# Macaron encoder on one core: the first operands of an FFN's second projection formed ahead of the last gate, and the joining copies moved one product later

## The chip, the cores and the metric

The kernel runs on one core of a Trainium2 chip. The metric is the time of one execution on the device in microseconds (us), lower is better. The core has five engines that run side by side, each through its own instructions in order: TensorE (PE in the profile; its weight loads are PEld), VectorE (DVE), ScalarE (ACT), GpSimd (POOL) and SyncE (SP), which issues DMAs. They wait for each other through semaphores.

## The reference

Two layers, each with two half-step FFNs around a mixer, then a final norm; all in float32, for 512 tokens of width 1024.

```python
def swiglu(x, w_in, w_out):            # w_in 1024 x 5632, w_out 2816 x 1024
    gu = x @ w_in
    g, u = jnp.split(gu, 2, axis=-1)
    return (jax.nn.silu(g) * u) @ w_out

for l in range(DEPTH):                 # DEPTH = 2
    x = x + 0.5 * swiglu(rms_norm(x, ffn1_norm[l]), ffn1_w_in[l], ffn1_w_out[l])
    x = x + mixer(rms_norm(x, mix_norm[l]), ...)
    x = x + 0.5 * swiglu(rms_norm(x, ffn2_norm[l]), ffn2_w_in[l], ffn2_w_out[l])
return rms_norm(x, final_norm)
```

So there are four FFN stages. The change touches these alone.

## The kernel before, in words

**Numbers as halves.** Every float32 operand is split into a high part and a low part that the tensor engine can take, and a product is three matmuls: high x high (L491 in the profile), low x high (L492), high x low (L494). A weight granule arrives by DMA as `raw` (128 x 1024). ACT copies it to its high half `whi` (L191, or L186 where the sign is turned), DVE subtracts to get the low half `wlo` (L194, L187). `whi` and `wlo` have three buffers each, so the making of a half waits until PE has read an older one. `ws.next()` hands a granule to a product and prepares those two places ahead. Weight loads are issued on SP eight granules ahead; some get a second weight added to them by a POOL DMA or by DVE (L164).

**Seven products instead of eight.** Matrix products are taken in 2 x 2 blocks by a Strassen scheme. In the first projection an FFN has five blocks of columns (`jb` 0 to 4). A block runs seven products on PE in this order, each two granules of 12 matmuls: A (operand 1), B (5), A (6), C (2), A (7), B (3), A (4). Between them ACT copies results from PSUM (`snap`, L561, tiles `sn`) and DVE subtracts (`less`, L566). `gate` forms the SwiGLU gate for one half of the tokens: ACT's tanh (L722, tiles `th`), one DVE product (L723); `times` (L729) multiplies by the other projection. `z1` is the gated tile of token half 0, ready behind the last product; `z2` that of half 1, ready a little before it.

**Turning.** The second projection needs the gated tiles with columns and rows exchanged. `halves` lets ACT copy a gated tile as 16-bit words into a buffer `zs` (two copies, L681) and SP issue a DMA transpose into `zt` (L682); the pair is put on the list `turned`. `joined` takes the first of the list and lets ACT copy its words from `zt` into a tile `at` (L698): two copies of 128 x 1024, or, where a block's four column tiles fall into two chunks, two of 128 x 256 and two of 128 x 768. The two tiles of a block are joined in the next block; those of the last block in the second projection.

**The second projection.** `at` has twelve tiles: two halves, two token halves, three chunks of 3, 4 and 4 column tiles. The list `steps` names 21 products on PE (tiles `o`), by operand 1 (three chunks), 2 (three), then for each chunk 5, 6, 7, 3, and last 4 (three). `make(i)` forms the operand of step i once: where a difference or sum of `at` tiles is needed DVE forms it in place (L742), ACT copies the high part `c1h`, `c2h`, ... (L321), DVE subtracts the low part `c1l`, ... (L322). Step i's loop pass calls `make(i)` and `make(i + 1)` ahead of its product and `make(i + 2)` behind it. Operands 1 of the first two chunks are made of tiles that the earlier blocks have filled; those of step 5 (operand 2, last chunk) and later need the last block's tiles. `update` (L748) adds finished products to x.

**Order.** Inside a stage most instructions are put in order by a scheduler that follows the order of the Python calls and the engines' estimated times; a place in the code is therefore a place in a priority order, and the built order can differ from it by a few instructions. Three of the four stages (all but the second) also load ACT's table for the square root at the end of the first projection.

Of the kernel before, what the change touches and what calls it, by code (L numbers as in the profile page):

```python
# [37 lines left out]
NB = 5  # L38
# [52 lines left out]
def encoder_kernel(  # L91
# [29 lines left out]
    def pair(s="ps"):  # L121
        return [bank(s), bank(s)]
# [373 lines left out]
    def product(ps, acts, kts, start, stop=True, again=False, hook=None, by_block=False, ahead=AHEAD):  # L496

        h, l, off = acts  # L500
        n = (len(kts) + 1) // 2

        def granule(i, w, b):
            res = []
            for k, kt in enumerate(kts[2 * i : 2 * i + 2]):
                c, z = slice(off + b * P, off + (b + 1) * P), slice(k * T, (k + 1) * T)
                res.append((
                    ps[b], h[:, kt, c], l[:, kt, c], w[0][:, z], w[1][:, z], start and i + k == 0,
                    stop and 2 * i + k == len(kts) - 1,
                ))  # L510
            return res

        if by_block:
            w = [ws.next() for _ in range(n)]
            for b in range(2):
                for i in range(n):
                    late_low(granule(i, w[i], b), again)
            return
        for i in range(n):
            w = ws.next(AHEAD if i < n - 1 and ahead else ahead)  # L520
            if i < n - 1:
                late_low(granule(i, w, 0) + granule(i, w, 1), again)
            else:
                late_low(granule(i, w, 0), again)
                late_low(granule(i, w, 1), again)
            if hook and i == 0:
                hook()
# [36 lines left out]
    def less(ps, t):  # L564
        for b in range(2):
            res = V.tensor_tensor(t[:, b, :], ps[b], t[:, b, :], ALU.subtract)  # L566
        return res
# [30 lines left out]
    def stage_ffn(norm, nxt, late):  # L598
# [75 lines left out]
        late_at, turned = [], []  # L674
# [12 lines left out]
        def joined():  # L687

            t, j, f0 = turned.pop(0)
            q = 0  # L690
            while q < 4:
                h, c, i = PLACE[f0 + q]
                n = 1
                while q + n < 4 and PLACE[f0 + q + n] == (h, c, i + n):
                    n += 1
                to = at_tile(h, j, c).bitcast(U16).rearrange("p i (t w) -> p w i t", w=2)
                for w in range(2):
                    S.activation(to[:, w, i : i + n, :], t[:, w, q : q + n, :], AF.Copy)  # L698
                q += n
# [163 lines left out]
        for jb in range(0 if first else 1, NB):  # L863
            f0 = 2 + 4 * jb
            if first and jb == 0:
                with tc.manual_schedule(engines={mybir.EngineType.DVE, mybir.EngineType.Activation}):
                    pa = pair("A")
                    product(pa, acts[1], K4, True)
                    for j in range(2):
                        t = snap(pcl[j])  # L870
                        pcl[j] = [t[:, 0, :], t[:, 1, :]]
                    s1 = snap(pa)
                    second(s1)
                    pb = pair("B")
                    product(pb, acts[5], K4, True)
                    sb = snap(pb)
                    norm.rstd()
            else:
                pa, pb, s1, sb = two(jb)
                settle_at()  # L880
                joined()
            product(pa, acts[6], K4, False, again=True)
            s2 = snap(pa)
            settle_at()
            if turned:
                joined()
            if jb or not first:
                second(s1)
            else:
                plain_out()  # L890
            z1 = gate(s1, 0)
            product(pa, acts[7], K4, False, again=True)
            less(pa, sb)
            product(pb, acts[3], K4, False, again=True)
            less(pb, s2)
            z2 = gate(s2, 1)
            times(z2, [sb[:, 0, :], sb[:, 1, :]], 1)
            halves(z2, 1, f0)
            if jb == NB - 1:
                make(0)  # L900
                make(1)
            product(pa, acts[4], K4, False, again=True)
            times(z1, pa, 0)
            halves(z1, 0, f0)
# [4 lines left out]
        for i, (m, c, _) in enumerate(steps):  # L909
            make(i)  # L910
            if i:
                make(i + 1)
            key = {6: 1, 4: 7}.get(m, m)
            if key not in ps:
                ps[key] = pair(f"o{key}")
            if m == 4 and c == 0 and nxt.mix:
                make(i + 2)
                ws.finish_stage()
                swap_pools(1)
            product(  # L920
                ps[key], made.pop(i), list(range(len(CHUNK[0][c]))), c == 0 and m in (1, 2, 3, 5, 7), c == 2,
                m in (4, 6), by_block=late and i == len(steps) - 1,
            )
            if i == 0:
                settle_at()
            if i == 1:
                turned.reverse()
                joined()
            if i == 3:
                joined()  # L930
            if m == 4 and c == 0 and not late:
                with tc.manual_schedule(engines={mybir.EngineType.DVE, mybir.EngineType.Activation}):
                    make(i + 2)
                    nxt.quad(1, 1)
                    if nxt.mix:
                        nxt.low01 = nxt.quad_high(0, 1)
                    else:
                        nxt.quad(0, 1)
            make(i + 2)
            if i == 6 and not late:  # L940
                nxt.quad(0, 0)
            if m == 4 and c == 1:
                update(ps[1], 1, 0, 1)
            if m == 4 and c == 0 and late:
                gf[0] = slot(F32, "gf", (D,))
                nc.sync.dma_start(out=gf[0], in_=bass.AP(tensor=gfin.tensor, offset=gfin.offset, ap=[[0, P], [1, D]]))
            if c < 2:
                continue
            if m == 1:
                update(ps[1], 0, 0, -1)  # L950
            elif m == 2:
                update(ps[2], 0, 0, 1)
                nxt.squares(0, 0)
            elif m == 5:
                update(ps[5], 0, 1, 1)
                update(ps[5], 1, 1, -1)
            elif m == 6:
                update(ps[1], 1, 1, 1)
            elif m == 7:
                update(ps[7], 1, 1, 1)  # L960
                nxt.squares(1, 1)
                update(ps[1], 0, 1, -1)
            elif m == 3:
                update(ps[3], 0, 1, 1)
                nxt.squares(0, 1)
                if late:
                    make(i + 3)
            elif late:
                with (
                    tc.issue_after(ws.items[-1].last.ins),  # L970
                    tc.manual_schedule(engines={mybir.EngineType.DVE, mybir.EngineType.Activation}),
                ):
                    ready = nxt.inverses(2)
                    next(ready)
                    gained(2, 0)
                    next(ready)
                    gained(2, 1)
                    for _ in ready:
                        pass
                    scaled(nxt, 2)  # L980
                    update(ps[7], 1, 0, 1, (0,))
                    nxt.squares(1, 0, (0,))
                    root = [nxt.inverse(b, *nxt.terms(b)) for b in range(2)]
                    next(root[0])
                    gained(3, 0)
                    gained(3, 1)
                    scaled(nxt, 3)
                    update(ps[7], 1, 0, 1, (1,))
                    nxt.squares(1, 0, (1,))
                    next(root[1])  # L990
                    next(root[0])
                    gained(0, 0)
                    next(root[0])
                    gained(0, 1)
                    scaled(nxt, 0)
                    next(root[1])
                    next(root[1])
                    whole(nxt, 1, 0)
                    whole(nxt, 1, 1)
            else:  # L1000
                update(ps[7], 1, 0, 1)
                if not nxt.mix:
                    nxt.squares(1, 0)
                nxt.later((1, 0))
# [978 lines left out]
```

## Time and profile before

| | |
|---|---|
| median of 3 runs | 1891.07 us (1890.44 to 1891.85) |
| the profiled execution | 1892.1 us |
| its span, first to last instruction | 1890.3 us |
| PE busy | 1860.5 us |
| DVE busy | 1641.4 us |
| ACT busy | 1310.0 us |
| mean granted clock of TensorE | 0.994 |

How to read it: times of a view are counted from the start of the span. A row of a timeline gives start, duration, engine, line, operation, what it writes and reads, shapes and how many such instructions the row joins; in brackets stands the idle time of that engine before it and what ended it. Matmuls overlap, so the distance between starts tells more than a duration. A row of stretches gives the stretch, its length, the busy time of PE, PEld, DVE, ACT and POOL with instruction counts, the granted clock, the DMA share and GB/s. A row of the waits gives who waited for whom, us in total, times, and the longest.

### The profile page before, as it was taken

The numbers are of one execution on the slowest core, as the hardware profiler recorded it, in microseconds if no ns is written. First come the engines' busy times: TensorE is split into PE (matmuls) and PEld (weight loads), VectorE is DVE, ScalarE is ACT, GpSimd is POOL, SyncE is SP. The second block draws the span as 40 slices with busy tenths as digits, with TensorE's granted clock in tenths as the row PEclk, the third lists the DMA queues.
The fourth block names the chain that finished last, engine by engine and source line by source line (L and its number), as shares of the span: only waits on it lengthen the run. The fifth ranks groups of instructions, "written<-read, shape, count | busy, mean of one in ns | idle before, by whom it ended". The sixth has DMA issues, their size and how long they took to land. (4 is left out here: it accounts for less than half of the span.)

```text
span 1890.3 us, 24637 instructions
## 1 busy us (share of the span) xinstructions
PE 1860.5 (98%) x8830; PEld 1549.5 (82%) x8830; DVE 1641.4 (87%) x2006; ACT 1310.0 (69%) x1788; POOL 171.3 (9%) x210
## 2 busy tenths in 40 slices
PE   9999999999999999999999999999999999999998
PEld 7888788888888888878888877888888888888786
DVE  7878899788989988879998878998989899887898
ACT  6777775668666767776667767666685576777764
POOL 0101011100111101001010100101001101000010
PEclk9999999999999999999999999999999999999999
DMA  9898799832886788879888886989248867888794
GB/s 299 223 244 202 194 254 280 213 104 93 249 224 163 182 211 231 206 201 265 251 186 226 209 211 181 267 265 211 84 134 232 214 172 175 229 215 206 197 273 153
DMA packets 190140, 393.70 MB, mean 208 GB/s; under 512 B 95489, under 2 KB 95617, under 8 KB 190017
## 3 DMA queue, kind: packets, MB, share of 16 engines
q1 hardware_dynamic: 161344, 293.77, 48.6%
q0 software_dynamic: 28528, 98.33, 28.9%
q8 instruction: 69, 1.13, 0.2%
q14 instruction: 55, 0.44, 0.1%
q10 hardware_dynamic: 144, 0.02, 0.0%
HBM read 365.85 MB, written 2.11 MB: 195 GB/s over the span
## 5 line engine op out<-in xcount | busy, mean ns | idle before, releaser
L194 DVE TENSOR_TENSOR wlo<-raw,whi 128x1024 fp32r<-128x1024 f32 (+1 forms) x534 | 631.1, 1195 | 166.8 <-ACT whi L191 165.7
L191 ACT ACTIVATE whi<-raw 128x1024 fp32r<-128x1024 f32 (+1 forms) x534 | 546.9, 1036 | 299.5 <-DVE raw L164 56.9
L150 POOL DMA_DIRECT2D raw<-in_wst_dram x166 | 144.3, 888 | 1400.5 <-DMA raw<-in_wst_dram 722.2
L164 DVE TENSOR_TENSOR raw<-raw,raw 128x1024 f32<-128x1024 f32 (+1 forms) x150 | 179.1, 1196 | 2.2
L492 PE MATMUL A<-whi,xl 128*128 128x512 f32 x400 | 155.7, 389 | 0.0
L491 PE MATMUL A<-whi,xh 128*128 128x512 f32 x400 | 155.7, 389 | 0.0
L698 ACT ACTIVATE at<-zt 128x1024 uint16<-128x1024 uint16 (+2 forms) x96 | 110.9, 1172 | 17.7 <-DMA zt<-zs 17.5
L186 ACT ACTIVATE whi<-raw 128x1024 fp32r<-128x1024 f32 (+1 forms) x83 | 86.0, 1037 | 48.5 <-PE A L492 21.5
L494 PE MATMUL A<-wlo,xh 128*128 128x512 f32 x400 | 115.0, 389 | 0.0
L187 DVE SCALAR_TENSOR_TENSOR wlo<-raw,whi 128x1024 fp32r<-128x1024 f32 (+1 forms) x83 | 98.6, 1197 | 15.5 <-ACT whi L186 15.3
L722 ACT ACTIVATE th<-sn,rh 128x512 f32<-128x512 f32 x80 | 55.7, 718 | 46.4 <-DVE sn L566 45.8
L494 PEld LDWEIGHTS A<-wlo,xh 128*128 128x128 f32 x400 | 75.1, 188 | 15.6
L491 PEld LDWEIGHTS A<-whi,xh 128*128 128x128 f32 x400 | 75.1, 188 | 15.4
L492 PEld LDWEIGHTS A<-whi,xl 128*128 128x128 f32 x400 | 75.1, 188 | 15.4
L491 PE MATMUL C<-whi,xh 128*128 128x512 f32 x208 | 82.1, 395 | 4.3 <-ACT whi L191 4.3
L492 PE MATMUL C<-whi,xl 128*128 128x512 f32 x208 | 81.7, 393 | 0.0
L492 PE MATMUL B<-whi,xl 128*128 128x512 f32 x208 | 81.0, 389 | 0.0
L491 PE MATMUL B<-whi,xh 128*128 128x512 f32 x208 | 80.9, 389 | 0.0
L681 ACT ACTIVATE zs<-th 128x1024 uint16<-128x1024 uint16 x80 | 79.6, 1043 | 0.4 <-DVE th L729 0.4
L561 ACT ACTIVATE sn<-A 128x512 f32<-128x512 f32 x104 | 59.3, 587 | 10.3 <-PE A L494 9.9
L494 PE MATMUL C<-wlo,xh 128*128 128x512 f32 x208 | 60.5, 393 | 0.0
L494 PE MATMUL B<-wlo,xh 128*128 128x512 f32 x208 | 59.8, 389 | 0.0
(449 smaller groups left out, 4790.3 us busy)
## 6 DMA issues: line engine op xcount, KB each, us to landing
raw<-in_wst_dram SPq DMA_DIRECT2D x470, 512.0 KB, 5.9
raw<-in_wst_dram POOLq DMA_DIRECT2D x174, 512.0 KB, 8.3
raw<-in_wst_dram SPq DMA_DIRECT2D x30, 256.0 KB, 3.5
bm<-in_bias_dram SPq DMA_DIRECT2D x16, 384.0 KB, 3.7
vs<-v SPq DMA_DIRECT2D x12, 256.0 KB, 3.8
x<-in_xin_dram SPq DMA_DIRECT2D x4, 512.0 KB, 10.2
raw<-in_wst_dram POOLq DMA_DIRECT2D x8, 256.0 KB, 8.1
dft<-in_dft_dram POOLq DMA_DIRECT2D x8, 256.0 KB, 4.4
```

The lines of the kernel that those rows point to most:

```text
L150: G.dma_start(out=self.t, in_=wst[GRAN_AT[self.plus]][:, 0 : self.n], accum_op=ALU.add)
L164: V.tensor_tensor(self.raw.t, self.raw.t, self.add.t, ALU.add)
L186: S.activation(hi, t, AF.Copy, scale=-1.0)
L187: self.last = V.scalar_tensor_tensor(lo, t, -1.0, hi.bitcast(F32), ALU.mult, ALU.subtract)
L191: S.activation(hi[:, cs], t[:, cs], AF.Copy)
L194: self.last = V.tensor_tensor(lo[:, cs], t[:, cs], hi[:, cs].bitcast(F32), ALU.subtract)
L491: PE.matmul(ps, lh, rh, start=start, stop=False, skip_group_check=again)
L492: PE.matmul(ps, ll, rh, start=False, stop=False, skip_group_check=again)
L494: PE.matmul(ps, lh, rl, start=False, stop=stop, skip_group_check=again)
L561: S.activation(t[:, b, :], ps[b], AF.Copy)
L681: S.activation(s[:, h], words[:, h], AF.Copy)
L698: S.activation(to[:, w, i : i + n, :], t[:, w, q : q + n, :], AF.Copy)
```

## The change

The call of `joined()` that stood behind the second product of a block is gone; the one behind the third product stays (it joins the first turned tile now), and a new one stands behind the fifth product, for the second tile. In the last block `make(0)` and `make(1)`, the operands of the first two steps of the second projection, move from behind `halves(z2, ...)` to ahead of `gate(s2, 1)`. The last block's two tiles are joined at steps 2 and 5 of the second projection instead of 1 and 3.

```diff
             else:
                 pa, pb, s1, sb = two(jb)
                 settle_at()
-                joined()
             product(pa, acts[6], K4, False, again=True)
             s2 = snap(pa)
             settle_at()
...
             z1 = gate(s1, 0)
             product(pa, acts[7], K4, False, again=True)
+            if turned:
+                joined()
             less(pa, sb)
             product(pb, acts[3], K4, False, again=True)
             less(pb, s2)
+            if jb == NB - 1:
+                make(0)
+                make(1)
             z2 = gate(s2, 1)
             times(z2, [sb[:, 0, :], sb[:, 1, :]], 1)
             halves(z2, 1, f0)
-            if jb == NB - 1:
-                make(0)
-                make(1)
             product(pa, acts[4], K4, False, again=True)
             times(z1, pa, 0)
             halves(z1, 0, f0)
...
             if i == 0:
                 settle_at()
-            if i == 1:
+            if i == 2:
                 turned.reverse()
                 joined()
-            if i == 3:
+            if i == 5:
                 joined()
```

## The prediction

> **What bounds the kernel now.** I read the page's first part, then who waited for whom on PE, then the timeline around the longest waits, then busy time by stretch of time.
>
> ```profile
> PE 1860.5 (98%) x8830; PEld 1549.5 (82%) x8830; DVE 1641.4 (87%) x2006; ACT 1310.0 (69%) x1788; POOL 171.3 (9%) x210
> PE o L491 <- ACT c1h L321: 13.5, 4, 3.4
> PE C L491 <- ACT whi L191: 4.3, 4, 2.3
> PE o L492 <- DVE c1l L322: 0.5, 2, 0.3
> ```
>
> PE is busy 98% of the span, so only its waits can be won. There are two families of four, one per FFN stage: the start of the second projection (o) waits for its first operand c1h, 13.5 us together, and a product C in the first projection waits for a weight half, 4.3 us. First one end of a first projection, on PE:
>
> ```profile
> 216.01 0.39 PE L491 MATMUL A<-whi,xh 128*128 128x512 f32 x1
> 218.73 0.39 PE L491 MATMUL A<-whi,xh 128*128 128x512 f32 x1
> 221.00 0.61 PE L494 MATMUL A<-wlo,xh 128*128 128x512 f32 x2
> 224.99 1.14 PE L491 MATMUL o<-whi,c1h 128*128 128x512 f32 x2 [3.37 <-ACT c1h L321]
> 229.55 0.40 PE L491 MATMUL o<-whi,c1h 128*128 128x512 f32 x1
> 222.00:226.00 4.00, 1.01 (x3) 0.44 (x3) 3.02 (x5) 4.00 (x6) 0.00 (x0) 0.89 0.47 158
> 226.00:232.00 6.00, 6.00 (x22) 4.90 (x22) 5.97 (x6) 5.97 (x7) 0.00 (x0) 0.79 1.07 227
> ```
>
> The last two rows are stretches of time; the figure behind the five busy times is the granted clock (0.89, 0.79). A granule of 12 matmuls takes 218.73 - 216.01 = 2.72 us. PE stands still for 3.37 us, and the 12 matmuls behind the wait take 229.55 - 224.99 = 4.56 us, because the clock is granted at half for a while. One end costs 3.37 + 1.84 = 5.2 us, four cost 20.8.
>
> Why c1h is late is seen on ACT, which works in order:
>
> ```profile
> 206.26 1.34 ACT L722 ACTIVATE th<-sn,rh 128x512 f32<-128x512 f32 x2 [0.32 <-DVE sn L566]
> 210.37 1.06 ACT L191 ACTIVATE whi<-raw 128x1024 fp32r<-128x1024 f32 x1 [1.81 <-issue]
> 212.58 1.06 ACT L191 ACTIVATE whi<-raw 128x1024 fp32r<-128x1024 f32 x1 [1.15 <-PE B L492]
> 221.25 1.06 ACT L186 ACTIVATE whi<-raw 128x1024 fp32r<-128x1024 f32 x1 [2.54 <-PE A L492]
> 222.21 1.99 ACT L681 ACTIVATE zs<-th 128x1024 uint16<-128x1024 uint16 x2
> 224.10 1.78 ACT L321 ACTIVATE c1h<-at 128x768 fp32r<-128x768 f32 x2
> 225.78 1.99 ACT L681 ACTIVATE zs<-th 128x1024 uint16<-128x1024 uint16 x2
> 227.79 1.28 ACT L907 ACT_TABLE_LOAD   x1
> 229.09 0.20 ACT L907 ACTIVATE sq<-ones 128x1 f32<-128x1 f32 x1
> 230.15 1.04 ACT L321 ACTIVATE c1h<-at 128x1024 fp32r<-128x1024 f32 x1
> 233.90 2.58 ACT L698 ACTIVATE at<-zt 128x1024 uint16<-128x1024 uint16 x2
> ```
>
> The two c1h, 1.78 us, stand behind the zs copies of the last gated tile, which itself is ready only when the product ends. They read tiles of earlier blocks.
>
> **The change part by part.**
>
> *Operands 0 and 1 ahead of the last gate.* In the built order the c1h now stand before the weight halves of the block's last product, their c1l on DVE directly behind the second `less`. The two at copies of the second turned tile (2.58 us) are also put into this stretch, from one product earlier. What hides these 4.4 us: ACT idles 1.81 + 1.15 us there, and the half started at 210.37 ends at 211.43 and is used at 216.01. Laid in a row behind th (ending 207.6): at, weight half, at, first c1h to 211.8, weight half to 212.8. Its lead shrinks from 4.6 to 3.2 us: no stall. If that cover were gone, each further us is a us of PE. On DVE:
>
> ```profile
> 213.68 1.23 DVE L194 TENSOR_TENSOR wlo<-raw,whi 128x1024 fp32r<-128x1024 f32 x1 [0.99 <-ACT whi L191]
> 217.28 1.23 DVE L187 SCALAR_TENSOR_TENSOR wlo<-raw,whi 128x1024 fp32r<-128x1024 f32 x1 [0.38 <-ACT whi L186]
> 224.97 0.96 DVE L322 TENSOR_TENSOR c1l<-at,c1h 128x768 fp32r<-128x768 f32 x1 [0.94 <-ACT c1h L321]
> 225.96 0.96 DVE L742 TENSOR_TENSOR at<-at,at 128x768 f32<-128x768 f32 x1
> 226.83 1.22 DVE L322 TENSOR_TENSOR c1l<-at,c1h 128x1024 fp32r<-128x1024 f32 x1
> 227.97 3.35 DVE L742 TENSOR_TENSOR at<-at,at 128x768 f32<-128x768 f32 x3
> ```
>
> The c1l (0.87 + 1.14 us from start to next start) fall into a stretch with idle gaps like those in the first two rows; carried along the order, the last gate's products on DVE end some 0.5 us later than now. All four waits of 3.37 us and their slow granules go: **20.8 us**.
>
> *What is late next.* The third c1h and c1l. PE would begin the projection at 221.45 (two matmuls of 0.227 us after 221.00) and need them after granules of 2.72, 1.36, 2.72 and 2.72 us, at 230.97; its built order starts with two matmuls of the high part, so the low part is needed at 231.4. ACT, in its new order: zs of z2 to 224.1, two weight halves to 226.45, zs of z1 to 228.35, table load and sq to 229.75, c1h to 230.8. DVE: behind the last gate's weights, the four subtractions L742 (4.0 us) and two weight lows end at 230.8, c1l at 232.1. A stall of 0.7 us. In the second FFN stage there is no table load, but one weight half and its low part stand ahead of c1l: 1.8 us. Three times 0.7 and once 1.8: **-3.9 us**. Whether 1.8 us of waiting brings the half clock is open: rows below bound it, 1.17 us without and 2.32 us with it; I take no half clock, as nearer to the first, and keep 1.84 us for the range. [...]
>
> [...]
>
> *The second projection can give some back.* DVE is nearly full there, and in the third stage its low halves already come just in time:
>
> ```profile
> 1180.00:1246.00 66.00, 66.00 (x297) 54.73 (x296) 63.25 (x64) 40.86 (x49) 8.63 (x10) 1.00 0.91 258
> 1792.00:1858.00 66.00, 66.00 (x293) 54.66 (x292) 64.75 (x65) 40.03 (x46) 8.59 (x10) 1.00 0.92 261
> 1251.07 1.23 DVE L194 TENSOR_TENSOR wlo<-raw,whi 128x1024 fp32r<-128x1024 f32 x1
> 1252.35 1.21 PE L494 MATMUL o<-wlo,c3h 128*128 128x512 f32 x4
> 313.19 1.23 DVE L194 TENSOR_TENSOR wlo<-raw,whi 128x1024 fp32r<-128x1024 f32 x1
> 315.69 0.61 PE L494 MATMUL o<-wlo,c3h 128*128 128x512 f32 x2
> ```
>
> DVE is busy 63.25 and 64.75 of 66 us (the third busy time). PE cannot come earlier than DVE does, plus the lead: 1.27 us in the first stage (314.42 to 315.69), 0.05 in the third. DVE itself comes earlier by the two c1l and the gap before them less the delay: 2.0 + 0.94 - 0.5 = 2.4 us, up to 3.8 with its small gaps. That lets the first stage keep its 4.5 us (5.2 - 0.7). The third keeps about 3.2, the fourth, with as full a DVE, I set alike: **-2.5 us**.
>
> *The at copies one product later.* In ordinary blocks they only change places with other copies: nothing. In the block behind the one whose tiles are split over two chunks:
>
> ```profile
> 1093.81 0.50 ACT L698 ACTIVATE at<-zt 128x256 uint16<-128x256 uint16 x1 [3.04 <-DMA zt<-zs]
> 1096.03 1.06 ACT L698 ACTIVATE at<-zt 128x768 uint16<-128x768 uint16 x1
> 1096.93 2.01 ACT L191 ACTIVATE whi<-raw 128x1024 fp32r<-128x1024 f32 x2
> 1098.04 0.50 PE L491 MATMUL C<-whi,xh 128*128 128x512 f32 x1 [2.32 <-ACT whi L191]
> 1711.24 0.50 PE L491 MATMUL C<-whi,xh 128*128 128x512 f32 x1 [1.17 <-ACT whi L191]
> 1090.00:1105.00 15.00, 12.68 (x49) 9.97 (x48) 6.78 (x6) 10.91 (x16) 0.00 (x0) 0.89 0.56 142
> ```
>
> ACT stands in line for a turned tile, then two long copies and two snaps come ahead of the weight half for C. The built order keeps the wait (the 256-wide copies stay), but puts the half before both long copies and the second snap: it comes 1.85 us sooner. The longest C wait falls from 2.32 to 0.5, its half clock goes (0.11 x 15 = 1.7 us), the other three, 4.3 - 2.3 = 2.0 us, vanish: 1.85 + 1.7 + 2.0 = **5.5 us**. Joining at steps 2 and 5 instead of 1 and 3 moves 2.58 us on ACT twice, before tiles that are needed steps later: nothing. On SP one weight load now stands between the last two transposes, and the later loads wait for a zs that ends 0.6 us later; they are fetched eight granules ahead: nothing.
>
> *Sum:* 20.8 - 3.9 - 2.5 + 5.5 = 19.9 us. The profiled execution took 1892.1 us (span 1890.3); less 19.9 is 1872.2. The median of the runs is 1.03 us lower: **1871**.
>
> **The rivals.**
>
> *Everything is kept* (DVE and ACT keep pace): 20.8 + 0.2 for c1l + 5.5 = 26.5 us, 1864.5. For it: what DVE lacks is under 2 us an end. Against: the 0.05 us lead.
>
> *DVE becomes the bound.* If the c1l only displace other DVE work ahead of the gate, DVE wins just its 0.94 us gap, and PE that plus its lead: 2.2 us in the first stage, the same assumed for the second, 1.0 in the other two, 6.4 in all, with 5.5 for C 11.9 us: 1879. If C gains only half, 1882. For it: 63 to 65 of 66 us busy. Against: the idle gaps before the gate.
>
> *Nothing to measure:* the built order puts the c1h where the text says, so this needs losses that happen to cancel the gains: 1891.
>
> *Slower.* Place: DVE's order ahead of the third c1l, where the four subtractions and the weight lows now stand. If that c1l comes x us after PE needs it, an end loses x + 1.84 (half clock again) for the 20.8 + 5.5 = 26.3 us won over four ends; it decides from x = 26.3 / 4 - 1.84 = 4.7 us. I work out 0.7 and 1.8. At x = 6 the kernel takes 1891 + 4 x 7.84 - 26.3 = 1896. For it: DVE has no idle left there. Against: no row makes 4 us more.
>
> **How the numbers follow.** Forecast 0.55; all kept 0.15; DVE bound 0.18; nothing 0.05; slower 0.07. A measurement of this kernel can tell about 0.2%, 3.8 us. The first three are faster by more: 0.88. The range takes these three with their ends: 1864 to 1882; what is left out is 0.12. The 1.84 us of the second stage lie inside.
>
> **What would show it.** Right: PE's waits for c1h gone, the granted clock full at each start of a second projection; a wait of PE for c1l of 0.5 to 2 us, longest in the second stage; C waits under 1 us; short waits of PE for wlo in the second projections of the third and fourth stage. Wrong: a wait of over 2 us at the third operand, PE waiting for wlo by several us (DVE bound), or a wait in the last two products of a first projection (ACT too full).

## The result, and the profile after

| | before | changed |
|---|---|---|
| median | 1890.76 us (1889.64 to 1891.85) | 1871.08 us (1869.66 to 1872.91) |
| the profiled execution | 1892.1 us | 1872.9 us |
| its span | 1890.3 us | 1871.1 us |
| ratio of the times | | 0.990, 95% 0.988 to 0.991 |

Faster by 1.0%, 19.7 us; 19.9 us were forecast, for 1871. The profiled execution of the changed kernel is the longest of its four (the other three spans were 1867.9 to 1869.4).

The profile's first part and the waits of PE, changed kernel:

```profile
PE 1854.5 (99%) x8830; PEld 1543.7 (82%) x8830; DVE 1638.3 (88%) x2006; ACT 1307.7 (70%) x1788; POOL 171.4 (9%) x210
```
```profile
PE A L491 <- ACT sn L561: 1.9, 2, 1.1
PE o L492 <- DVE c1l L322: 1.6, 3, 0.5
PE o L494 <- DVE wlo L194: 1.0, 2, 0.7
PE o L491 <- ACT c2h L321: 1.0, 1, 1.0
PE C L491 <- ACT whi L191: 0.5, 1, 0.5
```

The family c1h (13.5 us) is gone, the family C is down from 4.3 us to one wait of 0.5. In their place stand small waits: for the third operand (c1l, three times 0.5), for a weight's low half, and for the second family of operands (c2h, once). One start of a second projection, on PE, with the stretch around it:

```profile
220.73 0.62 PE L494 MATMUL A<-wlo,xh 128*128 128x512 f32 x2
221.19 0.39 PE L491 MATMUL o<-whi,c1h 128*128 128x512 f32 x1
223.91 0.39 PE L491 MATMUL o<-whi,c1h 128*128 128x512 f32 x1
```
```profile
221.00:227.00 6.00, 6.00 (x28) 4.99 (x27) 6.00 (x8) 5.60 (x6) 0.00 (x0) 1.00 0.62 180
```

No idle time, 2.72 us for the granule instead of 4.56, the granted clock 1.00.

Both kernels run 8830 matmuls, so the two traces can be laid over each other: start of PE's k-th matmul before, less that of the k-th after. Read over the stages, this shift tells where the 19.2 us of the spans came from (gain +, loss −):

| shift gained in stage | 1 | 2 | 3 | 4 | sum | forecast |
|---|---|---|---|---|---|---|
| around the product C | −0.35 | +0.6 | +4.1 | +1.4 | +5.7 | +5.5 |
| start of the second projection | +5.2 | +5.8 | +5.6 | +5.4 | +22.0 | +20.8 |
| third and fourth operand | −0.7 | −1.0 | −0.85 | −0.75 | −3.3 | −3.9 |
| given back later in the second projection | −2.3 | 0 | −2.15 | −0.26 | −4.7 | −2.5 |

The rest, −0.55 us, is +0.65 in the first 10 us of the span, and −0.8 and −0.4 where the two mixers begin: PE waits there for 0.75 and 1.10 us (the row "A <- sn" above; the kernel before had one such wait, of 0.86 us).

So the total was right, but not every term: the starts and C won a little more than worked out, and nearly twice as much was given back. Where the first stage gave it back is seen behind its third operand, on ACT, DVE and SP's queue in turn:

```profile
228.26 1.28 ACT L908 ACT_TABLE_LOAD   x1
229.55 0.20 ACT L908 ACTIVATE sq<-ones 128x1 f32<-128x1 f32 x1
229.66 1.05 ACT L321 ACTIVATE c1h<-at 128x1024 fp32r<-128x1024 f32 x1
232.29 1.04 ACT L191 ACTIVATE whi<-raw 128x1024 fp32r<-128x1024 f32 x1
236.51 1.37 ACT L698 ACTIVATE at<-zt 128x1024 uint16<-128x1024 uint16 x1 [3.17 <-DMA zt<-zs]
237.75 0.61 ACT L191 ACTIVATE whi<-raw 128x512 fp32r<-128x512 f32 x1
```
```profile
230.74 1.22 DVE L322 TENSOR_TENSOR c1l<-at,c1h 128x1024 fp32r<-128x1024 f32 x1 [0.65 <-ACT c1h L321]
238.39 0.69 DVE L194 TENSOR_TENSOR wlo<-raw,whi 128x512 fp32r<-128x512 f32 x1 [3.29 <-ACT whi L191]
```
```profile
224.26 5.09 SPq L682 DMA_TRANSPOSE zt<-zs  x1
229.44 0.53 SPq L148 DMA_DIRECT2D raw<-in_wst_dram  x1
230.07 3.38 SPq L682 DMA_TRANSPOSE zt<-zs  x1
```

ACT comes to the first joining copy at 233.3 and stands there 3.17 us for the turned tile (the list is reversed, so the tile that is joined first is the one turned last). The weight half behind it is 3.2 us late, and DVE idles 3.29 us for that half. In the kernel before, the copy at 233.90 did not wait at all: PE's stall had put ACT behind the transposes. Then, the two transposes stood back to back in the queue:

```profile
224.48 5.43 SPq L682 DMA_TRANSPOSE zt<-zs  x2
```

Here the one weight load between them, forecast at nothing, is in the way. In all four stages ACT stands for that tile, 3.17, 2.26, 1.06 and 0.80 us.

That standing alone does not give the size of what a stage loses (2.3, 0, 2.15 and 0.26 us). DVE's idle time for weight halves in the first 69 us of each second projection follows the loss better: it goes from 0.2, 0.3, 1.7 and 1.2 us in the kernel before to 3.6, 0.9, 3.7 and 1.1. In the third stage only 1.16 of the 3.7 us stand right behind the tile. The other 2.5 us stand behind two halves for which ACT waited for a weight load, as the 1.7 us of the kernel before do:

```profile
1204.71 1.06 ACT L191 ACTIVATE whi<-raw 128x1024 fp32r<-128x1024 f32 x1 [1.98 <-DMA raw<-in_wst_dram]
1208.75 2.01 ACT L191 ACTIVATE whi<-raw 128x1024 fp32r<-128x1024 f32 x2 [2.03 <-DMA raw<-in_wst_dram]
1209.85 1.23 DVE L194 TENSOR_TENSOR wlo<-raw,whi 128x1024 fp32r<-128x1024 f32 x1 [1.68 <-ACT whi L191]
```

Whether the tile made these loads later is not shown.

### The profile page after: what moved, and what is told of

It reads as the page before. It is cut to its first block, busy times and chain, and to the rows that moved or that the text cites. A ratio compares the mean times of both kernels' runs of the same rounds, so it can differ in the third digit from the quotient of the medians.

```text
span 1871.1 us, 24628 instructions
## 1 busy us (share of the span) xinstructions
PE 1854.5 (99%) x8830; PEld 1543.7 (82%) x8830; DVE 1638.3 (88%) x2006; ACT 1307.7 (70%) x1788; POOL 171.4 (9%) x210
## 4 chain that ended last, share of the span: by engine, by line
PE 85%; DVE 5%; DMA 5%; issue 4%; ACT 1%; POOL 0%; SPq 0%; DVEq 0%; ACTq 0%; POOLq 0%
PE A L491 10%; PE A L492 10%; PE A L494 10%; PE B L492 5%; PE B L491 5%; PE B L494 5%; PE o L494 5%; PE o L492 5%; PE o L491 5%; DMA raw<-in_wst_dram 4%; PE ps L315 3%; PE ps L316 3%; PE ps L317 3%; PE C L491 2%; PE C L492 2%
```

## The experiments

The theory to test: PE's stall at c1h, with its half clock, is what the change removes; joining later is needed to keep that gain; and what is given back is ACT's standing for the turned tile, which DVE, nearly full, cannot make up. Each run was set against the kernel before on the same chip (medians 1892.1 for the first four, 1892.7 for the next three, 1893.0 for the last two). The changed kernel was timed on another occasion, with 1890.8 for the kernel before, so a difference of under some 2 us between it and a run tells nothing.

| run | median us | ratio to before, 95% |
|---|---|---|
| changed kernel | 1871.1 | 0.990 (0.988 to 0.991) |
| e1 operands ahead alone | 1883.8 | 0.997 (0.995 to 0.999) |
| e2 later joins alone | 1884.4 | 0.996 (0.994 to 0.997) |
| e3 the wait filled | 1884.1 | 0.996 (0.994 to 0.997) |
| e4 changed, transposes back to back | 1867.1 | 0.9865 (0.985 to 0.988) |
| e5 changed, first join at step 3 | 1866.3 | 0.9865 (0.985 to 0.988) |
| e6 changed, DVE relieved | 1866.6 | 0.987 (0.985 to 0.9885) |
| e7 e4, third operand before the table load | 1867.6 | 0.987 (0.9855 to 0.9885) |
| e8 e5, third operand ahead of the gate | 1862.1 | 0.984 (0.9825 to 0.985) |
| e9 e4 and e5 together | 1866.0 | 0.986 (0.985 to 0.987) |

### e1: the operands ahead alone

```diff
             less(pb, s2)
+            if jb == NB - 1:
+                make(0)
+                make(1)
             z2 = gate(s2, 1)
...
             halves(z2, 1, f0)
-            if jb == NB - 1:
-                make(0)
-                make(1)
```

> Only the two operands move ahead of the last gate; the joining copies stay where they were. Theory (the operand move wins the starts of the second projections, the copies' move wins the C waits and keeps ACT free behind the start): the four waits for c1h go (22 us with their slow granules, less 3.3 us for the third operand), the C waits and their half clock stay (5.7 us not won). The last block's first tile is still joined ahead of c2h on ACT, and its transpose lands about 15 us behind the end of the first projection, so PE waits for c2h some 2.6 us in each stage, 10 us in all: about 1880 us. Rival (the two moves simply add): no new wait, 1891 - 22 + 3.3 + 4.7 given back = 1877 us.

Measured 1883.8: only 8.3 us (its ten runs took 1881.5 to 1896.9), less than theory and rival alike had forecast; a good part of what the starts win is lost again. The new waits are those that the theory named, but 4.6 us together and not 10, with smaller ones for c1l and c2l beside them. Waits of PE, and what stands behind the longest (PE, ACT, and a stretch of time):

```profile
PE o L491 <- ACT c2h L321: 4.6, 4, 2.1
PE o L492 <- DVE c1l L322: 2.6, 4, 1.0
PE o L492 <- DVE c2l L322: 1.9, 4, 0.5
```
```profile
239.29 0.55 PE L491 MATMUL o<-whi,c2h 128*128 128x512 f32 x1 [2.06 <-ACT c2h L321]
236.01 2.54 ACT L698 ACTIVATE at<-zt 128x1024 uint16<-128x1024 uint16 x2 [3.48 <-DMA zt<-zs]
238.42 0.81 ACT L321 ACTIVATE c2h<-at 128x768 fp32r<-128x768 f32 x1
```
```profile
236.00:246.00 10.00, 7.50 (x27) 5.52 (x26) 6.73 (x8) 9.99 (x11) 1.72 (x2) 0.83 0.84 211
```

The waits for c1h are gone, but with the join at step 1 the copy that stands for the tile lies ahead of c2h itself. In the first stage PE stalls 2.06 us and then has the half clock for (1 - 0.83) x 10 x 2 = 3.4 us. The shift against the kernel before, 0.34 us ahead of the start of that second projection, rises to 5.58 behind it and is back at 0.58 at 243 us: nearly nothing is kept in this stage. So the later join, which the prediction priced at nothing in the second projection, carries part of the gain.

### e2: the later joins alone

```diff
-                joined()                 # behind the second product
...
+            if turned:
+                joined()                 # behind the fifth product
...
-            if i == 1:
+            if i == 2:
...
-            if i == 3:
+            if i == 5:
```

> Only the joining copies move (in the blocks and at steps 2 and 5); the operands stay behind the last gate. Theory: the C waits of the split blocks shrink and their half clock goes, worth 5.5 to 5.7 us; the four waits of 3.4 us for c1h stay: 1885 to 1886 us. Rival (the later copies win nothing by themselves, the C waits are won by the earlier start of a stage): 1890 to 1891 us.

```profile
PE o L491 <- ACT c1h L321: 13.8, 4, 3.7
PE o L492 <- DVE c1l L322: 0.3, 1, 0.3
```

Measured 1884.4, 7.7 us: no wait for C is left, the four for c1h stand as before. The 5.5 us of the sum's C term were thus not too high. How much of it needs the later joins is less clear: in e1, where the joins are not moved, the third stage's wait for C is 0.50 us instead of 2.32, with the clock at full, and PE wins 3.5 us there against the kernel before.

The two parts alone give 8.3 + 7.7 = 16.0 us, together 19.7. That each is worth more with the other fits the waits for c2h in e1, but the times do not show it: by the intervals the first part is worth 2 to 10 us, the second 5 to 11.

### e3: the wait filled

```diff
             product(pa, acts[4], K4, False, again=True)
+            if jb == NB - 1:
+                for _ in range(14):
+                    PE.matmul(pb[0], hx[1][:, 0, 0:P], hx[1][:, 1, :], start=True, stop=True)
             times(z1, pa, 0)
```

> The kernel before with 14 extra matmuls into an unused bank behind the last product of each first projection, so PE works through most of its wait for c1h. Their results are used nowhere. Theory (the slow granules behind the wait come from PE having stood idle): c1h comes as late as before, but the first granule takes 2.7 to 2.8 us instead of 4.56, and no half clock is granted at the four starts: 1.8 us each, 7 us in all, less what DVE takes back in the second projections (up to 3 us): 1884 to 1887 us. Rival (the granule is slow because its own operands c1l and whi come late): the granule stays at 4.5 us and the time at 1891 us.

This is the kernel before, with 14 matmuls of no use into a bank that is free, where PE would wait for c1h. PE, and a stretch:

```profile
222.91 3.33 PE L905 MATMUL B<-xh 128*128 128x512 f32 x14
226.45 0.73 PE L491 MATMUL o<-whi,c1h 128*128 128x512 f32 x2 [0.20 <-ACT c1h L321]
229.85 0.39 PE L491 MATMUL o<-whi,c1h 128*128 128x512 f32 x1
```
```profile
226.00:232.00 6.00, 5.53 (x24) 4.08 (x23) 5.50 (x6) 5.97 (x8) 0.00 (x0) 1.00 1.24 199
```

Measured 1884.1, 8.0 us less with c1h as late as ever. The granted clock is 1.00 at all four starts (0.998 as the mean of the execution, 0.994 in the kernel before): the half clock at these starts follows from PE's idling and not from what c1h waits for. The granule takes 229.85 - 226.45 = 3.40 us for 4.56, 0.26 us of it a wait for c1l; the 2.7 to 2.8 us expected did not come. Laid over the kernel before, PE wins 1.2, 1.6, 1.4 and 1.1 us at the four starts, 5.2 us in all and not 4 x 1.84 = 7.4. So the median's 8.0 us are not these granules alone. In the profiled execution, the longest of the four (5.2 us less than the kernel before), the third stage's C wins 3.0 us, and the first stage's loses 2.1 by this wait:

```profile
162.89 0.50 PE L491 MATMUL C<-whi,xh 128*128 128x512 f32 x1 [2.42 <-ACT whi L191]
155.00:175.00 20.00, 17.57 (x78) 14.20 (x77) 11.90 (x12) 15.28 (x21) 1.22 (x2) 1.00 0.66 177
```

That wait is longer than the 2.06 us of e1 and the 2.32 us of the kernel before, and no half clock follows.

### e4: the transposes back to back

The weight load that stands between the two last transposes on SP is issued behind the second; the order of ACT, DVE and PE is that of the changed kernel. `hold` keeps the loads from the fourth on behind that transpose; the lines that hand the transpose on and end the hold at step 1 are left out here.

```diff
+                    hold[1] += 1
+                    with tc.issue_after(hold[0]) if hold[0] and hold[1] > 3 else nullcontext():
+                        nc.sync.dma_start(out=self.t[:, cs], in_=wst[GRAN_AT[self.key]][:, cs])
...
-            halves(z1, 0, f0)
+            turn = halves(z1, 0, f0)     # the last transpose
+            if jb == NB - 1:
+                hold[:] = [turn, 0]
```

> The changed kernel with one thing put back on SP: the weight load that stands between the last two transposes of each stage comes behind both. All other engines keep their order. Theory (that load, and the transpose's wait for it, makes the last turned tile land late; ACT stands in line for it 3.17 us in the first stage, DVE behind it 3.3 us, and the second projection then lacks what DVE did not do): the tile lands some 2.5 us sooner, ACT's wait in the first stage falls under 1 us, and the first stage gives back 1 us or less instead of 2.3: 1869 us. Rival (DVE is full in the second projection anyway): ACT waits less, PE's waits only change place, 1871 us.

SP's queue, and the copy that waited 3.17 us:

```profile
222.96 7.02 SPq L686 DMA_TRANSPOSE zt<-zs  x2
230.08 6.38 SPq L152 DMA_DIRECT2D raw<-in_wst_dram  x5
233.54 1.37 ACT L703 ACTIVATE at<-zt 128x1024 uint16<-128x1024 uint16 x1 [1.50 <-DMA zt<-zs]
```

Measured 1867.1, 4.0 us under the changed kernel, 2 us more than expected (the two profiled executions differ by 5.7 us, of which 1.1 lie ahead of the first place that the edit touches). ACT's standing fell to 1.50 and 0.37 us in the first two stages and is gone in the others. "On SP one weight load now stands between the last two transposes", set at nothing, was a wrong step.

### e5: the first join at step 3

```diff
-            if i == 2:
+            if i == 3:
                 turned.reverse()
                 joined()
```

> The changed kernel with the last block's first tile joined at step 3 of the second projection instead of step 2. In the changed kernel ACT stands in line for that tile for 3.17, 2.26, 1.06 and 0.80 us in the four stages, and DVE then idles for weight halves 3.6, 0.9, 3.7 and 1.1 us in the first 69 us of a second projection. Theory (ACT's standing for a tile is what the second projections give back): one product later the tile has landed, these idle times mostly go, and the first and third stage give back about 2 us less each: 1867 to 1868.5. Rival (the two ordinary loads on SP beside the transposes cost it in another way, or DVE is full anyway): 1870.5 to 1871.5 with ACT's waits gone.

```profile
235.70 2.58 ACT L698 ACTIVATE at<-zt 128x1024 uint16<-128x1024 uint16 x2 [2.04 <-DMA zt<-zs]
```

Measured 1866.3, a little under the theory's range, by one figure in the code. SP's order is not touched here, and the tile comes late in the first stage still (the wait is 2.04 us), but one more weight half and a c2h lie ahead of it now. How full DVE and PE are in 69 us at the start of the second projections, first and third stage, changed kernel and then e5 (the first number behind the length is PE, the third DVE):

```profile
221.00:290.00 69.00, 68.02 (x299) 54.58 (x298) 64.79 (x66) 50.12 (x59) 8.60 (x10) 1.00 0.97 249
1152.00:1221.00 69.00, 68.47 (x304) 55.72 (x303) 64.66 (x64) 48.80 (x58) 10.28 (x12) 1.00 1.00 269
```
```profile
221.00:290.00 69.00, 68.48 (x306) 56.25 (x305) 66.60 (x67) 51.12 (x60) 9.47 (x11) 1.00 1.02 264
1152.00:1221.00 69.00, 68.48 (x305) 56.23 (x305) 68.12 (x68) 50.85 (x59) 10.24 (x12) 1.00 1.03 279
```

DVE works 66.6 and 68.1 of the 69 us, for 64.8 and 64.7. Laid over the changed kernel, e5's PE wins 1.7 us inside the first second projection and 2.4 in the third, and 0.8 and 1.5 us where the mixers begin, with the waits of 0.75 and 1.10 us gone; a wait of 0.54 us for wlo in the last projection takes some back. A further 1.1 us of the difference of the two profiled executions lies ahead of the edit (mostly in the first 10 us and at C of the first stage) and is not of its making.

### e6: DVE relieved

```diff
         def summed(self):
-            if self.add:
+            if self.add and self.raw.key[1][0] != "o":
                 V.tensor_tensor(self.raw.t, self.raw.t, self.add.t, ALU.add)
```

> The changed kernel without the additions of a second weight on DVE (L164) in the second projections, so products 6 and 3 there use one weight alone: DVE has 7 to 10 instructions of 1.08 us less per stage. Theory (DVE, 93 to 98% busy there, cannot make up what ACT's late weight halves cost it): with the slack DVE makes it up, PE's waits for wlo go, and the starts in each stage are kept: 1864 to 1867. Rival (PE loses the time directly to ACT's late halves, DVE's load is no bound): 1870 to 1871.5 with the same waits.

The groups of DVE's weight low halves in the stretch 225 to 290 us, changed kernel and then e6 (busy, mean, then the idle time ahead of them), and the waits of PE in e6:

```profile
L194 DVE TENSOR_TENSOR wlo<-raw,whi 128x1024 fp32r<-128x1024 f32 (+1 forms) x22 | 23.9, 1096 | 3.6 <-ACT whi L191 3.6
```
```profile
L194 DVE TENSOR_TENSOR wlo<-raw,whi 128x1024 fp32r<-128x1024 f32 (+1 forms) x23 | 25.1, 1101 | 4.6 <-ACT whi L191 4.6
```
```profile
PE o L492 <- DVE c1l L322: 1.6, 3, 0.5
PE o L491 <- ACT c2h L321: 1.0, 1, 1.0
```

Measured 1866.6. ACT stands for the tile much as before (2.4, 2.2 and 1.7 us in three stages) and DVE idles even longer for the halves behind it, 4.6 us; but with 12 additions fewer in each second projection (1958 instructions for 2006; e6 leaves out the second weight that products 6 and 3 need) it has the time to make that up, and PE's waits for wlo are gone. So that DVE is full is part of why ACT's late halves cost PE time: this is the "DVE becomes the bound" rival, in part. Its 4.5 us are not a pure price of DVE's load: PE's order is that of the changed kernel, but ACT's and DVE's differ in places, and ACT no longer waits for these additions (14.5 us between 225 and 330 us in the changed kernel).

### e7 and e8: the third operand earlier, in two places

In e7, on e4, behind the copies of z1; in e8, on e5, ahead of the last gate.

```diff
             turn = halves(z1, 0, f0)
             if jb == NB - 1:
                 hold[:] = [turn, 0]
+        make(2)                          # e7

         if late or nxt.mix:
```
```diff
             if jb == NB - 1:
                 make(0)
                 make(1)
+                make(2)                  # e8
             z2 = gate(s2, 1)
```

> The reordered kernel of the run before (weight load behind both last transposes; 1867.1) with the third operand made right behind the copies of z1, ahead of the square root's table load. Theory (the third operand's wait is c1h's place on ACT, behind the table load of 1.28 us): its c1l waits of 0.5 us go in three stages, 1865.5 to 1866.5 where the second projection keeps them. Rival (c1l is held by DVE's four subtractions ahead of it, or the gain is given back): 1867 to 1867.5, with the c1l waits as they were.

> The kernel with the first join at step 3 (1866.3) with the third operand, too, formed ahead of the last gate. Theory (what is left are waits: 0.52 us for c1l in three stages, 0.97 for c2h in one): the c1l waits go, 1863.5 to 1865.5. Rival (DVE, with 1.14 us more ahead of the gate, brings the last product's gate or weight low parts late, or gives it back later): c1l waits gone, but waits in the last two products or for c2, 1866.3 or more.

Waits of PE in e7, and DVE there ahead of c1l:

```profile
PE o L496 <- DVE c1l L326: 3.3, 3, 1.1
```
```profile
229.07 1.22 DVE L191 SCALAR_TENSOR_TENSOR wlo<-raw,whi 128x1024 fp32r<-128x1024 f32 x1
230.20 1.21 DVE L326 TENSOR_TENSOR c1l<-at,c1h 128x1024 fp32r<-128x1024 f32 x1
```

e7 came to nothing, 1867.6 for 1867.1. c1h moved ahead of the table load, but a weight half moved with it and ahead of it, and on DVE that half's low part now stands ahead of c1l: PE waits 1.1 us for 0.5. The rival's guess, DVE's order, was the right one, with one weight low more in it than it named.

In e8 c1l is done before the gate. All waits of PE in the projections that are left, and the stretches of the first and third stage:

```profile
PE o L494 <- DVE wlo L194: 0.6, 1, 0.6
```
```profile
221.00:290.00 69.00, 69.00 (x310) 57.23 (x309) 68.00 (x69) 51.23 (x60) 10.35 (x12) 1.00 1.00 277
1152.00:1221.00 69.00, 69.00 (x310) 57.23 (x309) 68.64 (x70) 47.51 (x56) 10.26 (x12) 1.00 0.97 275
```

1862.1: 4.2 us under e5, where 0.8 to 2.8 were expected, and 1.6% under the kernel before. PE starts 310 matmuls in these 69 us, for 299 and 304 in the changed kernel, and DVE still keeps pace at 68.0 and 68.6 of 69 us. The 1.57 + 0.97 us of waits for c1l and c2h were not the whole price: laid over e5, the shift grows by 0.7 to 0.9 us at each c1l and 1.3 at the c2h, so some of the matmuls around such a wait must come late too without a wait being shown; the rest is spread over the second projections.

### e9: e4 and e5 together

> Both reorderings together: the weight load behind both last transposes and the first join at step 3. Alone they gave 1867.1 and 1866.3 for 1871.1 of the changed kernel. Theory (both take away the same thing, ACT's standing for the turned tile, of which the join at step 3 leaves 2.0 us in the first stage): not additive, 1865.5 to 1866.5. Rival (the load between the transposes costs something of its own, 4 us): 1862 to 1863.

Measured 1866.0, the theory's value, not 1862. This fits two edits that take away the same thing, and the load between the transposes adds no 4 us of its own on top of e5. A common floor would look alike, though: e4, e5, e6 and e9 all end at 1866 to 1867, with the same waits for c1l and c2h left, and only e8, without these waits, goes below.

## Why the prediction was right

- *The starts* (+20.8; measured +22.0): the step held as worked out, 5.2 us in the first stage to the tenth. ACT and DVE took the c1h and c1l where the text put them, with no wait in the last two products.
- *The slow granules* inside that term are shown by e3: with PE at work through the wait the granted clock is 1.00 at all four starts, so it is PE's idling that costs them. In e1 a wait of 2.06 us was followed by 3.4 us at half clock, as one of 2.32 us was in the trace of before; one of 2.42 us in e3 was not, so the length of a wait does not decide alone. The stall that the prediction took without the half clock stayed at 0.98 us and at full clock (1.00 from 832 to 901 us).
- *The third operand* (−3.9; measured −3.3): c1l late by 0.53 us in three stages, for 0.7 forecast. In the second stage, where the text looked for the longest wait for c1l, none came; the fourth operand, c2h, was late there, by 0.98 us for 1.8. The four subtractions, the slower case's place, did not add more.
- *The table load* started at 228.26 and took 1.28 us, and ACT's next instruction, started at 229.55, ended at 229.75: to the hundredth where the sum for the third operand had it.
- *C* (+5.5; measured +5.7): the third stage won 4.1 us for 3.55; in the first stage one wait of 0.54 us stayed (before, 0.36), so the three small ones did not all vanish. In e2 and in e4 to e9, with the joins of the blocks moved alike, none is left. What won the 4.1 us is in part open: e1 wins 3.5 us at that place without the moved joins.
- *Given back* (−2.5; measured −4.7): the mis-sized term. The first stage was to keep all and gave back 2.3 us, the third gave 2.15 for 1.3, the fourth 0.26 for 1.2. The step that failed is not the lead of DVE, but two that were set to nothing: the joining copies at steps 2 and 5, "before tiles that are needed steps later", and the weight load between the transposes. The tile is indeed needed steps later; but the weight half behind the copy on ACT came 3.2 us late with it in the first stage, and DVE stood idle 3.29 us for it. With PE's stall gone there was no longer anything to hide the transposes. e4 and e5 each take this away, in part or whole, and gain 4.0 and 4.8 us, not additive (e9). DVE's lead of 0.05 us, the reason given for the third stage's loss, did not bind there: in e5 that stage gives nothing back behind its third operand. What the late weight loads add to that stage's loss stays open. The short waits for wlo came in the first and third stage (0.3 and 0.7 us), not in the third and fourth.

The errors went in both directions, +1.4 for the starts and C together, +0.6 for the third operand, −2.2 for what is given back and −0.55 for the rest, and nearly cancelled; that the total is within 0.1 us of the median is luck, more than the steps earned.

## What to carry to other kernels

When a stall of the bounding engine goes, list what finished under its cover: here two DMA transposes, whose landing ACT waited for by 0.4 us at most while PE stood still. The copy that waited for a DMA was dear here by what was queued behind it on its engine (e4 and e5, 4.0 and 4.8 us), not by when its own result was needed; put such a copy behind everything that is ready, up to the last place that its reader allows (step 3 for the tile that step 5 reads). And operands whose inputs are ready early are better formed before the last gate altogether than squeezed in behind it: e7 and e8 move the same operand, for nothing (on e4) and for 4.2 us (on e5).

## What the runs showed of the hardware

- A wait of 2.06 us (e1, with one of 0.44 us behind it) and one of 2.32 us (before) were each followed by 3.4 us at half clock; waits of 1.17 us (before, granted clock 1.00) and 2.42 us (e3, first stage, granted clock 1.00) were not, nor were the 2.38 us in all that PE stood idle from 1163 to 1173 us in e1 (third stage, granted clock 1.00). So no length of a wait separates the two, and what does was not shown.
- In the trace of the kernel before, the half clock (granted clock 0.50) comes in five stretches of 3.41 us, and once more at the end of the span. They begin at 225.1, 836.1, 1098.9, 1163.8 and 1774.8 us, the third behind the wait of 2.32 us, the others behind the four waits of 3.37 us for c1h. In the changed kernel it comes at the end of the span alone.
- The last two transposes of a stage held SP's queue for 3.3 to 5.1 us each where a weight load stood between them (changed kernel), and for 5.4 to 6.8 us (before) or 7.0 us (e4, first stage) together where they stood back to back. In the first stage it took from the end of the copies into zs to the landing of the second tile 8.3 us with the load between (changed kernel) and 6.6 without (e4). Whether the load itself or the other transfers in flight cost that time was not told apart.
